# A SwiGLU down projection as seven block products in place of eight, and a zero fill on another queue

## The chip, the cores and the metric

One Trainium2 chip, one of its cores. The metric is the device time of the whole kernel in microseconds. A NeuronCore has five engines with a queue each: PE (TensorE, matmuls), DVE (VectorE), ACT (ScalarE), POOL (GpSimd) and SP (SyncE, which here only issues DMAs). ACT can issue DMAs too. PE writes into PSUM, which has eight banks of 128 x 512 floats; DVE and ACT take results out of it.

## The reference

Two transformer-like blocks follow each other on x, 1024 tokens by 1024 features, in float32. The first mixes by retention (8 heads) and a state space branch (S5), then by cross attention to 256 memory rows. The second mixes by four small mixers, one of them a gated delta rule, and ends in a SwiGLU layer and a norm. The change touches the last layer and, for its preparation, the retention:

```python
def swiglu(h, w_gate_up, w_down):
    gu = h @ w_gate_up
    gate, up = jnp.split(gu, 2, axis=-1)
    return (jax.nn.silu(gate) * up) @ w_down

x = x + swiglu(rmsnorm(x, norm2_w), w_gate_up, w_down)
return rmsnorm(x, final_norm_w)
```

The hidden width is 2816 = 22 x 128, so w_down has 2816 rows and 1024 columns.

## The kernel before, in words

**Products.** Every float32 operand of a large product is split into a high part (rounded to the matmul's format by ACT, L166, L181, L768) and a low part (the rest, by DVE, L167, L182, L769). `mm3` (L185) makes high x high, high x low and low x high, three matmuls (L187, L188, L189) of 128 x 128 weights by 512 columns, into one PSUM bank. Raw weights come through a ring of three buffers (`wraw`), the parts through rings of four (`whi`, `wlo`).

**Order.** Python generators are woven into each other and so give the order in which instructions are written down. From this, a scheduler with a model of the times makes a fixed order for each engine. An engine then takes its instructions in that order and waits at each for its semaphores; so do the DMA queues of SP and ACT.

**Retention** (L1097 and on). 32 steps m (four pairs of heads by eight chunks) interleave projections (`keys`, `values`), a transpose (`turn`), scores and outputs. At m = 0, 8, 16 and 24 `gates` (L1134) first makes two gate columns and loads the projection weights of the pair through `wraw`. The scan of the S5 branch (L1462 to L1464), a chain of small DVE instructions, runs beside it. At the start a zeroed tile is written to a DRAM buffer `t_d` by two DMAs of ACT's queue (L1112), each reading one tile of 129 columns 32 times. `t_d` is used far later, by the delta rule.

**Gate-up.** The product with w_gate_up is itself made of seven block products (`pair`, L802, with sums of weights from `prep`, L762, which is drawn one pair ahead; an even i is a gate, an odd i an up column pair). `finish` (L732) applies Silu to the gates (ACT), multiplies the up columns with them (POOL, L738) and stores the result, the hidden layer, to DRAM (`ff_d`, L740), 44 stores by SP.

**Down** (L842 to L878). The residual is loaded to `xk` (L843, eight DMAs of ACT's queue). The loop runs over f, two blocks of 128 rows of w_down at a time, 11 rounds. A round loads two blocks of the hidden layer (L849) and two of w_down (L177) by SP and splits them; then for each of 8 token tiles t and 2 halves c4 of the columns it makes 6 matmuls into a bank and adds the bank to `xk` (DVE, L864). In the last round each half is followed by a square with a row sum (ACT, L868) and the norm: POOL's power (L289), scaling by ACT (L876) and DVE (L877), and the output's DMA (L878).

Of the kernel before, what the change touches and what calls it, by code (L numbers as in the profile page):

```python
# [18 lines left out]
P = 128  # L19
# [103 lines left out]
class Kern:  # L123
# [482 lines left out]
    def stage2(self, x_d):  # L606
# [28 lines left out]
        ff_d = self.dram.tile([DFF, S], F32, name="ff_d")  # L635
# [96 lines left out]
        def finish(i, n, src):  # L732

            if i % 2 == 0:
                act.activation(src, src, AF.Silu)
                sg[n] = src
                return
            g.tensor_mul(src, src, sg[n])  # L738
            c, h = i // 2 * 2 + int(n[0]) - 1, int(n[1]) - 1
            nc.sync.dma_start(ff_d[c * P:(c + 1) * P, hs(h)], src)  # L740
# [7 lines left out]
        def add(i, n, other):  # L748

            def res(ps):  # L750
                tag, bufs = ("sg", 4) if i % 2 == 0 else ("nt" if i >= NEARLY else "sum", 2)
# [50 lines left out]
        def pair(i, w):  # L802
# [9 lines left out]
            yield from product(w["s2"], "t2", lambda ps: v.tensor_add(u2, ps, s1[i]))  # L812
            yield from product(w["s3"], "t3", lambda ps: v.tensor_add(u3, ps, u2))
# [17 lines left out]
        for i in range(NPAIR):  # L831
# [3 lines left out]
            self.drain(pair(i, w))  # L835
            w = w2


        NFT = 2
        fa = ArenaPool(self.slot(3, [P, 8192]), 2)  # L840
# [3 lines left out]
        for f0 in range(0, NF, NFT):  # L844
            fs = fa.tile([P, 2, NFT, S], F32R, tag="ff")
            ws = []
            for f in range(f0, f0 + NFT):
                r = self.wp.tile([P, S], F32, tag="wraw", name=self.nm("fraw"), bufs=3)
                nc.sync.dma_start(r, ff_d[f * P:(f + 1) * P])  # L849
                self.split(fs[:, 0, f - f0], fs[:, 1, f - f0], r)  # L850
                ws.append(self.weights([wd[f * P:(f + 1) * P]], 1))
            if f0 + NFT == NF:
                gb = self.wp.tile([P, NH, HT], F32, tag="wraw", name="gb", bufs=3)
                nc.scalar.dma_start(gb, I["final_norm_w_2"].rearrange("(o n c) -> o n c", o=1, n=NH).to_broadcast([P, NH, HT]))
            for t in range(KD):
                tok = slice(t * P, (t + 1) * P)
                if f0 + NFT == NF:
                    ms = self.wk.tile([P, 2], F32, tag="fms", name=self.nm("fms"))
                for c4 in range(2):
                    x = xk[:, t, c4]  # L860
                    ps = (self.pmm if c4 else pb).tile([P, HT], F32, tag="mm" if c4 else "b", name=self.nm("mm"))
# [1350 lines left out]
```

## Time and profile before

| what | us |
|---|---|
| median of 3 runs | 2501.27 (2499.54 to 2502.29) |
| the profiled execution, device time | 2498.12 |
| its span, first to last instruction | 2496.1 |
| PE busy in the span | 2418.4 (97%) |
| DVE, ACT, POOL busy | 1528.8, 827.3, 593.5 |
| mean granted TensorE clock | 0.989 of full speed |

All rows come from the profiled execution, whose times count from its first instruction. A row of the timeline gives start, duration, engine and line, what is written and read, and in brackets how long the engine stood idle before and what released it. "issue" as a releaser is time in which the engine waited for nothing that the profile shows. Tile names are those of the program; an arena has the name of its slot (s). A q behind an engine (SPq, ACTq) is its queue of DMA issues and semaphores.

### The profile page before, as it was taken

The numbers are of one execution on the slowest core, as the hardware profiler recorded it, in microseconds if no ns is written. First come the engines' busy times: TensorE is split into PE (matmuls) and PEld (weight loads), VectorE is DVE, ScalarE is ACT, GpSimd is POOL, SyncE is SP. The second block draws the span as 40 slices with busy tenths as digits, with TensorE's granted clock in tenths as the row PEclk, the third lists the DMA queues.
The fourth block names the chain that finished last, engine by engine and source line by source line (L and its number), as shares of the span: only waits on it lengthen the run. The fifth ranks groups of instructions, "written<-read, shape, count | busy, mean of one in ns | idle before, by whom it ended". The sixth has DMA issues, their size and how long they took to land.

```text
span 2496.1 us, 34790 instructions
## 1 busy us (share of the span) xinstructions
PE 2418.4 (97%) x13241; PEld 2026.5 (81%) x13241; DVE 1528.8 (61%) x2782; ACT 827.3 (33%) x1289; POOL 593.5 (24%) x538
## 2 busy tenths in 40 slices
PE   7998989999999999999999999999989999999998
PEld 7886779999977788888777788977868888888886
DVE  6456668934512775545785654367687666657777
ACT  6434311112112443444554322165443223221113
POOL 0006512322200441124635511043111111110002
PEclk9999999999999999999999999999999999999999
DMA  9745572112697444453346564236343222234332
GB/s 252 225 95 168 162 113 68 61 42 85 203 295 213 149 135 136 145 184 102 97 137 188 151 179 131 92 124 217 92 149 101 95 80 78 87 129 150 101 101 85
DMA packets 421382, 336.80 MB, mean 135 GB/s; under 512 B 46848, under 2 KB 364752, under 8 KB 420384
## 3 DMA queue, kind: packets, MB, share of 16 engines
q1 hardware_dynamic: 378960, 291.05, 38.5%
q10 hardware_dynamic: 42256, 43.52, 6.3%
q8 instruction: 105, 1.72, 0.3%
q14 instruction: 61, 0.50, 0.1%
HBM read 239.00 MB, written 95.52 MB: 134 GB/s over the span
## 4 chain that ended last, share of the span: by engine, by line
PE 80%; DVE 7%; DMA 4%; POOL 4%; issue 3%; ACT 2%; ACTq 1%; SPq 1%; POOLq 0%; DVEq 0%
PE mm L187 20%; PE mm L188 19%; PE mm L189 19%; PE qkv L187 3%; PE qkv L188 2%; PE qkv L189 2%; POOL m L1394 2%; PE yps L1085 1%; PE yps L1081 1%; DMA y<-y_d 1%; DVE wlo L182 1%; PE dz L2131 1%; DVE nt L308 1%; DVE s L310 1%; PE o L1200 1%
## 5 line engine op out<-in xcount | busy, mean ns | idle before, releaser
L187 PE MATMUL mm<-s,whi 128*128 128x512 f32 (+1 forms) x2112 | 833.9, 397 | 16.9 <-ACT sg L1137 6.3
L188 PE MATMUL mm<-s,whi 128*128 128x512 f32 (+1 forms) x2112 | 827.4, 392 | 2.2 <-DVE s L310 1.1
L189 PE MATMUL mm<-s,wlo 128*128 128x512 f32 (+1 forms) x2112 | 826.3, 392 | 2.2 <-DVE wlo L769 2.2
L187 PEld LDWEIGHTS mm<-s,whi 128*128 128x128 f32 x2112 | 400.8, 190 | 105.0 <-issue 6.9
L189 PEld LDWEIGHTS mm<-s,wlo 128*128 128x128 f32 x2112 | 401.4, 190 | 86.5 <-DVE wlo L769 3.5
L188 PEld LDWEIGHTS mm<-s,whi 128*128 128x128 f32 x2112 | 402.0, 190 | 82.4 <-issue 3.0
L182 DVE TENSOR_TENSOR wlo<-wraw,whi 128x1024 fp32r<-128x1024 f32 x204 | 280.4, 1376 | 184.1 <-ACT whi L181 179.5
L181 ACT ACTIVATE whi<-wraw 128x1024 fp32r<-128x1024 f32 x204 | 215.0, 1056 | 369.2 <-PE mm L188 197.7
L864 DVE TENSOR_TENSOR s<-mm,s 128x512 f32<-128x512 f32 x176 | 118.3, 688 | 66.9 <-PE mm L189 66.9
L738 POOL TENSOR_TENSOR c<-c,c 128x512 f32<-128x512 f32 x44 | 69.4, 1580 | 367.5 <-DVE c L753 213.8
L187 PE MATMUL mm<-whi,s 128*128 128x512 f32 (+1 forms) x416 | 155.3, 374 | 0.0
L188 PE MATMUL mm<-wlo,s 128*128 128x512 f32 (+1 forms) x416 | 155.2, 373 | 0.0
L189 PE MATMUL mm<-whi,s 128*128 128x512 f32 (+1 forms) x416 | 154.9, 373 | 0.0
L187 PE MATMUL qkv<-whi,s 128*128 128x256 f32 x512 | 152.2, 298 | 0.0
L188 PE MATMUL qkv<-wlo,s 128*128 128x256 f32 x512 | 147.5, 288 | 0.0
L189 PE MATMUL qkv<-whi,s 128*128 128x256 f32 x512 | 146.8, 287 | 0.0
L289 POOL TENSOR_TENSOR rs<-rv,mhalf 128x4 f32<-128x4 f32 (+3 forms) x47 | 49.2, 1047 | 228.8 <-DVE rv L287 212.5
L187 PEld LDWEIGHTS qkv<-whi,s 128*128 128x128 f32 x512 | 97.5, 190 | 4.7 <-issue 3.9
L768 ACT ACTIVATE whi<-wraw 128x1024 fp32r<-128x1024 f32 (+1 forms) x62 | 55.7, 907 | 135.5 <-PE mm L188 70.5
L188 PEld LDWEIGHTS qkv<-wlo,s 128*128 128x128 f32 x512 | 97.6, 191 | 0.9
L189 PEld LDWEIGHTS qkv<-whi,s 128*128 128x128 f32 x512 | 97.6, 191 | 0.3
L188 PEld LDWEIGHTS mm<-wlo,s 128*128 128x128 f32 x416 | 78.4, 188 | 13.8
(498 smaller groups left out, 3754.3 us busy)
## 6 DMA issues: line engine op xcount, KB each, us to landing
wraw<-in_w_in_dram SPq DMA_DIRECT2D x58, 512.0 KB
wraw<-in_w_out_dram SPq DMA_DIRECT2D x48, 512.0 KB
wraw<-in_w_gate_up_dram SPq DMA_DIRECT2D x48, 512.0 KB
ff_d<-c SPq DMA_DIRECT2D x44, 256.0 KB
fraw<-ff_d SPq DMA_DIRECT2D x22, 512.0 KB
wraw<-in_w_down_dram SPq DMA_DIRECT2D x22, 512.0 KB
s<-ret_d SPq DMA_DIRECT2D x16, 512.0 KB
s<-x_d SPq DMA_DIRECT2D x16, 512.0 KB
```

The costliest lines, as they stand in the source:

```text
L181: nc.scalar.activation(hi, raw, AF.Copy)
L182: nc.vector.tensor_sub(lo, raw, hi.bitcast(F32))
L187: mm(ps, ah, bh, start=start, stop=False)
L188: mm(ps, ah, bl, start=False, stop=False)
L189: mm(ps, al, bh, start=False, stop=stop)
L289: nc.gpsimd.tensor_tensor(r, v, self.mhalf[:, :1].to_broadcast([P, n]), op=ALU.pow)
L308: nc.vector.scalar_tensor_tensor(t[:, :n], src(k), g[:, k:k + 1], rb[:, :n], op0=ALU.mult, op1=ALU.mult)
L310: nc.vector.tensor_sub(lo[:, k, :n], t[:, :n], hi[:, k, :n].bitcast(F32))
L738: g.tensor_mul(src, src, sg[n])
L768: act.activation(d[0][:, s], src, AF.Copy)
L864: v.tensor_add(x, ps, x)
L1394: eng.tensor_tensor(out, a, b, op=ALU.mult)
```

## The change

Down is made of seven products of blocks instead of eight. w_down is cut by even and odd blocks of 128 rows and by halves of columns, the hidden layer by even and odd blocks and halves of tokens. Four sums of weights per pair of blocks (`down_sums`) are made by DVE during the retention, 11 steps, at the m listed in the diff, through the `wraw` ring, and stored to DRAM. Four sums of the hidden layer (t1 to t4) are made by DVE in the gate-up stage, after the third product of the pair that follows (`up_sums`), and stored by SP with three of the plain blocks, 77 stores in all. The new loop has the products outermost; each goes over 11 blocks in 6 steps (five of two blocks, one of one) and holds four PSUM banks, one per token tile of a half. Every step's operands are loaded from DRAM by SP and split (`down_loads`); two steps are kept ready, the first two before the last gate-up pair is over. `evac` adds each product to the outputs it belongs to. The norm's parts are made when a half is complete, for half of the tokens after the fifth product, for the others in the last, whose final two steps run tile by tile. The zero fill goes to SP, in eight DMAs at odd m from 5 on, from a tile of 1032 columns. The SBUF kept for descriptors of POOL's DMAs is set to 1024 bytes.

```diff
@@ -632,7 +632,8 @@
         self.wk = self.pool("wk2", 2)
         pt, pb = mx.pt, mx.pb
         xk_d = self.dram.tile([S, D], F32, name="xk_d")
-        ff_d = self.dram.tile([DFF, S], F32, name="ff_d")
+        ff_d = {n: self.dram.tile([DFF // 2 // P, P, HT], F32, name=f"ff_{n}")
+                for n in ("b11", "b21", "b22", "t1", "t2", "t3", "t4")}
         b_d = self.dram.tile([4, P, HT], F32, name="b_d")
         def turn_x(h):
@@ -736,8 +737,26 @@
                 sg[n] = src
                 return
             g.tensor_mul(src, src, sg[n])
-            c, h = i // 2 * 2 + int(n[0]) - 1, int(n[1]) - 1
-            nc.sync.dma_start(ff_d[c * P:(c + 1) * P, hs(h)], src)
+            up[i, n] = src
+            if n == "12":
+                pend.append(i)
+            else:
+                nc.sync.dma_start(ff_d["b" + n][i // 2], src)
+        up, pend = {}, []
+        def up_sums():
+            while pend:
+                i = pend.pop()
+                b11, b12, b21, b22 = (up.pop((i, n)) for n in ("11", "12", "21", "22"))
+                t2 = self.wk.tile([P, HT], F32, tag="ut2", name=self.nm("ut2"), bufs=1)
+                v.tensor_sub(b11, b12, b11)
+                v.tensor_sub(b12, b22, b12)
+                v.tensor_sub(t2, b22, b11)
+                v.tensor_sub(b21, b21, t2)
+                for n, t in (("t1", b11), ("t2", t2), ("t3", b12), ("t4", b21)):
+                    nc.sync.dma_start(ff_d[n][i // 2], t)
         def first(i, ps):
             tag = ("ssq0", "ssq1", "sq", "sq")[i % 4]
@@ -748,7 +767,7 @@
         def add(i, n, other):
             def res(ps):
-                tag, bufs = ("sg", 4) if i % 2 == 0 else ("nt" if i >= NEARLY else "sum", 2)
+                tag, bufs = ("sg", 4) if i % 2 == 0 else ("u" + n, 2 if n == "11" else 1)
                 c = self.wk.tile([P, HT], F32, tag=tag, name=self.nm("c"), bufs=bufs)
                 v.tensor_add(c, ps, other)
                 finish(i, n, c)
@@ -810,6 +829,7 @@
                 add(i, "22", u3)(ps)
                 v.tensor_add(u2, ps, u2)
             yield from product(w["s2"], "t2", lambda ps: v.tensor_add(u2, ps, s1[i]))
+            up_sums()
             yield from product(w["s3"], "t3", lambda ps: v.tensor_add(u3, ps, u2))
             yield from product(w["a22"], "t4", add(i, "21", u3))
             yield from product(w["s1"], "t1", fifth)
@@ -832,50 +852,115 @@
             if i + 1 < NPAIR:
                 w2 = prep(i + 1)
                 w2["rest"]()
-            self.drain(pair(i, w))
+            todo = pair(i, w)
+            if i + 1 == NPAIR:
+                self.drain(islice(todo, 4))
+                ld = self.down_loads(ff_d, wd)
+                ops = [next(ld) for _ in range(2)]
+            self.drain(todo)
             w = w2
-
-
-        NFT = 2
-        fa = ArenaPool(self.slot(3, [P, 8192]), 2)
+        up_sums()
+        self.down(ld, ops, xk_d, (self.pmm, "mm"), (pb, "b"), (pt, "tr"))
+    DOWN = (("a11", "b11"), ("a12", "b21"), ("s2", "t2"), ("s3", "t3"), ("a22", "t4"), ("s1", "t1"), ("s4", "b22"))
+    def down_loads(self, ff_d, wd):
+        nc = self.nc
+        ta = ArenaPool(self.slot(3, [P, 8192], F32))
+        wj = wd.rearrange("(j i p) (n c) -> i n p j c", i=2, p=P, n=2)
+        sw = self.sw_d.rearrange("i j p n c -> i n p j c")
+        at = {"a11": wj[0, 0], "a21": wj[0, 1], "a12": wj[1, 0], "a22": wj[1, 1],
+              "s2": sw[0, 0], "s3": sw[0, 1], "s4": sw[1, 0], "s1": sw[1, 1]}
+        for wn, xn in self.DOWN:
+            for j0 in range(0, 11, 2):
+                n = min(2, 11 - j0)
+                r = ta.tile([P, 2, HT], tag="traw", name=self.nm("traw"), bufs=2)[:, :n]
+                nc.sync.dma_start(r, ff_d[xn][j0:j0 + n].rearrange("j p c -> p j c"))
+                t = ta.tile([P, 2, 2, HT], F32R, tag="ts", name=self.nm("ts"), bufs=3)
+                raw = self.wp.tile([P, 2, HT], F32, tag="wraw", name=self.nm("wraw"), bufs=3)[:, :n]
+                nc.sync.dma_start(raw, at[wn][:, j0:j0 + n])
+                hi, lo = (self.wp.tile([P, 2, HT], F32R, tag=q, name=self.nm(q), bufs=4)[:, :n] for q in ("whi", "wlo"))
+                self.split(t[:, 0, :n], t[:, 1, :n], r)
+                self.split(hi, lo, raw)
+                yield t[:, 0], t[:, 1], hi, lo, n
+    def down(self, ld, ops, xk_d, *banks):
+        nc, v, act, g = self.nc, self.nc.vector, self.nc.scalar, self.nc.gpsimd
         xk = self.slot(2, [P, KD, NH, HT], F32)
         for t in range(KD):
             nc.scalar.dma_start(xk[:, t], xk_d[t * P:(t + 1) * P].rearrange("p (n c) -> p n c", n=NH))
-        for f0 in range(0, NF, NFT):
...
+        ac = Arena(self.slot(1, [P, 8192], F32))
+        gb, s1, u3 = ac.take((NH, HT)), ac.take((4, HT)), ac.take((4, HT))
+        nc.scalar.dma_start(gb, self.ins["final_norm_w_2"].rearrange("(o n c) -> o n c", o=1, n=NH).to_broadcast([P, NH, HT]))
+        ms = {}
+        def done(t, c):
+            x = xk[:, t, c]
+            last = t in ms
+            if not last:
+                ms[t] = ac.take((2,))
+            jk = self.wk.tile([P, HT], F32, tag="sg", name=self.nm("jk"), bufs=4)
+            act.activation(jk, x, AF.Square, accum_out=ms[t][:, c:c + 1])
+            if not last:
+                g.tensor_tensor(x, x, gb[:, c], op=ALU.mult)
+                return
+            m = self.wk.tile([P, 1], F32, tag="fm", name=self.nm("fm"))
+            v.tensor_add(m, ms[t][:, 0:1], ms[t][:, 1:2])
+            r = self.rstd_from(m, 1, 1.0 / D, "lrs")
+            act.activation(xk[:, t, 1 - c], xk[:, t, 1 - c], AF.Copy, scale=r)
+            v.scalar_tensor_tensor(x, x, r, gb[:, c], op0=ALU.mult, op1=ALU.mult)
+            nc.sync.dma_start(self.out[0, t * P:(t + 1) * P].rearrange("p (n c) -> p n c", n=NH), xk[:, t])
+        def add(t, c, other, last=True):
+            v.tensor_add(xk[:, t, c], other, xk[:, t, c])
+            if last:
+                done(t, c)
+        def evac(p, t, ps):
+            if p == 0:
+                act.activation(s1[:, t], ps, AF.Copy)
+                add(t, 0, s1[:, t], False)
+            elif p == 1:
+                add(t, 0, ps)
+            elif p == 2:
+                v.tensor_add(s1[:, t], ps, s1[:, t])
+            elif p == 3:
+                v.tensor_add(u3[:, t], ps, s1[:, t])
+                add(t, 1, u3[:, t], False)
+                add(t + 4, 1, u3[:, t], False)
+            elif p == 4:
+                add(t, 1, ps)
+            elif p == 5:
+                add(t + 4, 1, ps)
+                v.tensor_add(s1[:, t], ps, s1[:, t])
+                add(t + 4, 0, s1[:, t], False)
+            else:
+                add(t + 4, 0, ps)
+        NSTEP = 6
+        for p in range(len(self.DOWN)):
+            bank = [banks[0], banks[1], banks[2], banks[p % 2]]
+            ps = [b.tile([P, HT], F32, tag=tag, name=self.nm("mm")) for b, tag in bank]
+            def mms(t, i, op):
+                th, tl, wh, wl, n = op
                 tok = slice(t * P, (t + 1) * P)
...
+                for k in range(n):
+                    self.mm3(ps[t], th[:, k, tok], tl[:, k, tok], wh[:, k], wl[:, k], i == 0 and k == 0, i == NSTEP - 1 and k == n - 1)
+            final = p + 1 == len(self.DOWN)
+            for i in range(NSTEP - 2 * final):
+                op = ops.pop(0)
+                for t in range(4):
+                    mms(t, i, op)
+                ops += [o for o in [next(ld, None)] if o]
+            for t in range(4):
+                if final:
+                    for i, op in enumerate(ops):
+                        mms(t, NSTEP - 2 + i, op)
+                evac(p, t, ps[t])
 @@ -1106,11 +1191,15 @@
         self.load_consts(r1, "causalT", "inv")
         self.t_d = self.dram.tile([2, 8, 4, P + 1, P], F32, name="t_d")
-        zero = r1.tile([P, P + 1], F32, name="zero")
+        zero = r1.tile([P, 8 * (P + 1)], F32, name="zero")
         g.memset(zero, 0.0)
-        for i in range(2):
-            nc.scalar.dma_start(self.t_d[i].rearrange("n h s c -> (n h s c)").rearrange("(p a b) -> p a b", p=P, b=P + 1),
-                                zero.unsqueeze(1).to_broadcast([P, 32, P + 1]))
+        def zeros():
+            for i in range(2):
+                for n in range(0, 8, 2):
+                    nc.sync.dma_start(self.t_d[i, n:n + 2].rearrange("n h s c -> (n h s c)").rearrange("(p b) -> p b", p=P), zero)
+                    yield
+        zeros = zeros()
         cosb = r1.tile([P, 8, 32], F32, name="cosb")
         sinb = r1.tile([P, 8, 2, 32], F32, name="sinb")
         with ExitStack() as c:
@@ -1242,6 +1331,7 @@
                 for i, t in enumerate((hi, lo)):
                     nc.sync.dma_start(ret_d[i, ch * P:(ch + 1) * P, h * HT:(h + 1) * HT], t.bitcast(F32))
+        sums = self.down_sums()
         M = 32
         for m in range(M + 1):
             if m < M:
@@ -1258,8 +1348,30 @@
                 turn(m)
             if m and m % 4 == 0:
                 finish(m // 4 - 1)
+            if m % 2 and 5 <= m:
+                next(zeros, None)
+            if m in (10, 11, 12, 13, 14, 18, 19, 20, 21, 22, 26):
+                next(sums)
             if m == 29:
                 reload()
+    def down_sums(self):
+        nc, v = self.nc, self.nc.vector
+        wd = self.ins["w_down_2"][0]
+        self.sw_d = self.dram.tile([2, 11, P, NH, HT], F32, name="sw_d")
+        for j in range(11):
+            e, o = (self.wp.tile([P, NH, HT], F32, tag="wraw", name=self.nm("wdr"), bufs=3) for _ in range(2))
+            for i, t in enumerate((e, o)):
+                f = 2 * j + i
+                nc.sync.dma_start(t.rearrange("p n c -> p (n c)"), wd[f * P:(f + 1) * P])
+            v.tensor_add(o[:, 1], e[:, 1], o[:, 1])
+            v.tensor_sub(e[:, 1], e[:, 0], e[:, 1])
+            v.tensor_sub(e[:, 0], o[:, 1], e[:, 0])
+            v.tensor_sub(o[:, 0], o[:, 0], e[:, 0])
+            for i, t in enumerate((e, o)):
+                nc.sync.dma_start(self.sw_d[i, j], t)
+            yield
 
     def cmul(self, eng, o, a, b, t, conj_sign=1):
@@ -2196,7 +2308,7 @@
     import concourse.bacc as bacc
     from concourse.bass_utils import run_bass_kernel_spmd
-    nc = bacc.Bacc("TRN2", target_bir_lowering=False, num_devices=1)
+    nc = bacc.Bacc("TRN2", target_bir_lowering=False, num_devices=1, dynamic_dma_scratch_size=1024)
     consts, cols = shape_constants()
     arrays, aps = {}, {}
     for name in _INS + ["consts"]:
```

## Rows read from the trace of the kernel before

**Rows 1.** the page's first part: busy us (share of the span) and instructions
```profile
PE 2418.4 (97%) x13241; PEld 2026.5 (81%) x13241; DVE 1528.8 (61%) x2782; ACT 827.3 (33%) x1289; POOL 593.5 (24%) x538
```

**Rows 2.** groups by line, 2220 to 2500 us: busy us, mean ns | idle before, releaser
```profile
L188 PE MATMUL mm<-wlo,s 128*128 128x512 f32 x352 | 137.1, 389 | 0.0
L864 DVE TENSOR_TENSOR s<-mm,s 128x512 f32<-128x512 f32 x176 | 118.3, 688 | 66.9 <-PE mm L189 66.9
L167 DVE TENSOR_TENSOR s<-fraw,s 128x1024 fp32r<-128x1024 f32 x22 | 26.8, 1216 | 2.9 <-ACT s L166 2.9
```

**Rows 3.** timeline of PE, first and last matmul of the down stage: start us, us, ...
```profile
2245.39 0.39 PE L187 MATMUL mm<-whi,s 128*128 128x512 f32 x1
...
2484.53 0.39 PE L189 MATMUL mm<-whi,s 128*128 128x512 f32 x1
```

**Rows 4.** timeline of ACT, 295 to 370 us (ACTq: its DMA queue)
```profile
309.94 14.70 ACTq L1112 DMA_DIRECT2D t_d<-zero  x2
324.69 1.06 ACT L181 ACTIVATE whi<-wraw 128x1024 fp32r<-128x1024 f32 x1 [16.80 <-issue]
339.27 1.57 ACT L1137 ACTIVATE sg<-mm 128x512 f32<-128x512 f32 x3 [6.98 <-issue]
```

**Rows 5.** DMA in all, 661 to 680 us: loads of x_d and w_out
```profile
DMA packets 5937, 5.58 MB, mean 294 GB/s; under 512 B 160, under 2 KB 4239, under 8 KB 5936
```

**Rows 6.** timeline: two loads of 512 KB and the ACT instruction that each released
```profile
2235.29 0.32 SPq L849 DMA_DIRECT2D fraw<-ff_d  x1
2246.01 1.06 ACT L166 ACTIVATE s<-fraw 128x1024 fp32r<-128x1024 f32 x1 [11.23 <-DMA fraw<-ff_d]
...
2443.29 0.33 SPq L177 DMA_DIRECT2D wraw<-in_w_down_dram  x1
2447.09 1.06 ACT L181 ACTIVATE whi<-wraw 128x1024 fp32r<-128x1024 f32 x1 [3.60 <-DMA wraw<-in_w_down_dram]
```

**Rows 7.** timeline of all engines at the end, 2484 to 2497 us
```profile
2489.60 0.61 ACT L868 ACTIVATE jk<-s 128x512 f32<-128x512 f32 x1
2491.69 0.75 DVE L877 SCALAR_TENSOR_TENSOR s<-s,rs,gb 128x512 f32<-128x512 f32 x1 [0.72 <-POOL rs L289]
```

**Rows 8.** stretches: us, PE, PEld, DVE, ACT, POOL busy (x), PEclk, DMA share, GB/s
```profile
1945.00:2050.00 105.00, 105.00 (x464) 86.99 (x464) 68.12 (x89) 32.45 (x47) 14.24 (x10) 1.00 0.26 81
```

**Rows 9.** groups by line and shape, DVE, 1830 to 2224 us
```profile
L769 DVE TENSOR_TENSOR wlo<-a,whi 128x512 fp32r<-128x512 f32 x22 | 23.8, 1081 | 0.1
L769 DVE TENSOR_TENSOR wlo<-wraw,whi 128x512 fp32r<-128x512 f32 x22 | 15.0, 682 | 0.0
```

**Rows 10.** waits, 1830 to 2224 us: in total us, times, longest
```profile
DVE a L783 <- DMA wraw<-in_w_gate_up_dram: 35.5, 19, 2.9
```

**Rows 11.** timeline of PE, 316 to 348 us, around the two gaps
```profile
323.14 0.39 PE L189 MATMUL mm<-s,wlo 128*128 128x512 f32 x1
326.29 0.76 PE L187 MATMUL mm<-s,whi 128*128 128x512 f32 x1 [2.76 <-ACT g L479]
333.25 0.39 PE L189 MATMUL mm<-s,wlo 128*128 128x512 f32 x1
339.92 0.79 PE L187 MATMUL mm<-s,whi 128*128 128x512 f32 x1 [6.28 <-ACT sg L1137]
```

**Rows 12.** stretches, as Rows 8, of the retention's start
```profile
340.00:345.00 5.00, 5.00 (x15) 3.98 (x16) 4.26 (x18) 0.84 (x2) 0.00 (x0) 0.66 1.16 186
```

**Rows 13.** DMA queue of ACT, 332 to 339.3 us: packets, MB, share of 16 engines
```profile
q10 hardware_dynamic: 1069, 0.55, 69.1%
```

**Rows 14.** timeline of all engines, 446 to 457 us, one step of the retention
```profile
449.77 0.28 DVE L1182 TENSOR_TENSOR qk<-tr,consts 128x128 f32<-128x128 f32 x1
450.84 0.60 PE L1189 MATMUL sc<-qk 128*128 128x256 f32 x2
```

**Rows 15.** timeline of ACT, 400 to 530 us, one step m apart
```profile
452.24 0.38 ACT L1170 ACTIVATE vs<-qkv 128x256 f32<-128x256 f32 x1 [5.48 <-PE qkv L189]
460.07 0.38 ACT L1170 ACTIVATE vs<-qkv 128x256 f32<-128x256 f32 x1 [7.45 <-PE qkv L189]
```

More of the change, by code (lines that the diff above doesn't have):

```diff
@@ L843, in stage2 @@
             nc.scalar.dma_start(xk[:, t], xk_d[t * P:(t + 1) * P].rearrange("p (n c) -> p n c", n=NH))
-        for f0 in range(0, NF, NFT):
[L845 to L855, printed above, removed]
-                tok = slice(t * P, (t + 1) * P)
[L857 to L861, printed above, removed]
-                    for f, (wh, wl) in enumerate(ws):
-                        self.mm3(ps, fs[:, 0, f, tok], fs[:, 1, f, tok], wh[:, 0, hs(c4)], wl[:, 0, hs(c4)], f == 0, f == NFT - 1)
-                    v.tensor_add(x, ps, x)
-                    if f0 + NFT < NF:
-                        continue
-                    jk = self.wk.tile([P, HT], F32, tag="sg", name=self.nm("jk"), bufs=4)
-                    act.activation(jk, x, AF.Square, accum_out=ms[:, c4:c4 + 1])
-                    if c4 == 0:
-                        g.tensor_tensor(x, x, gb[:, c4], op=ALU.mult)
-                if f0 + NFT < NF:
-                    continue
-                m = self.wk.tile([P, 1], F32, tag="fm", name=self.nm("fm"))
-                v.tensor_add(m, ms[:, 0:1], ms[:, 1:2])
-                r = self.rstd_from(m, 1, 1.0 / D, "lrs")
-                act.activation(xk[:, t, 0], xk[:, t, 0], AF.Copy, scale=r)
-                v.scalar_tensor_tensor(xk[:, t, 1], xk[:, t, 1], r, gb[:, 1], op0=ALU.mult, op1=ALU.mult)
-                nc.sync.dma_start(self.out[0, tok].rearrange("p (n c) -> p n c", n=NH), xk[:, t])
```

## The prediction

> **What bounds the kernel now.** I read the page first: PE is busy 97% of the span [rows 1], so the question in each stage is which PE time goes and whether anything else becomes late. The groups of the last stage, the down projection, come next [rows 2]: three matmul lines of 352 each, 1056 in all, with no idle time in front of them, while DVE waits 66.9 us for PE in its sum out of PSUM (L864). PE sets the pace there. The timeline gives the pace: from 2245.39, the first start, to 2484.53, the last, are 1055 steps [rows 3], so (2484.53 - 2245.39) / 1055 = 0.2267 us per matmul (a row's 0.39 us overlaps the next one's). The stage ends with a stretch that has no matmul: the last one is over at 2484.53 + 0.39 = 2484.92, the span at 2496.1, so 11.2 us follow, in which DVE, ACT and POOL catch up on norms that came faster than they could be served, and the last output lands.
>
> **The products.** Before, 22 blocks of f, 8 token tiles, 2 halves and 3 matmuls make 1056. After, 7 products, 11 blocks, 4 token tiles and 3 make 924, of the same shape (128x128 by 512). 132 fewer at 0.2267 us: **-29.9 us**, the whole stage 209.5 us instead of 239.4, if PE stays the bound.
>
> Can the operands come in time? A step (two blocks, 24 matmuls) takes 5.44 us, and with the short sixth step the 42 steps take 209.5 / 42 = 4.99 us on average. For it ACT makes two high parts of 1.06 us [rows 4], DVE two low parts of 1.22 us [rows 2]. Per product DVE has 11 x 1.22 = 13.4 us of these and at most 12 sums of 0.69 us (8.3 us), 21.7 of 29.9 us. Bytes: 7 x 11 x 512 KB = 40.4 MB in 209.5 us, 193 GB/s. The loads of x_d and w_out, most of them in packets under 2 KB, ran at 294 GB/s [rows 5]. The tight place is the ring of two raw buffers: a buffer turns round in issue 0.33 + landing L + ACT 1.06 + DVE 1.22, so the ring gives a step every (2.6 + L) / 2 us and holds PE up where L is over 7.4 us. A 512 KB load landed in 3.8 us (2443.29 to 2447.09) beside one other load, and in 10.7 us (2235.29 to 2246.01) beside the 4 MB of the residual xk [rows 6]. I take 3.8 us for the stage, 3.2 us per step, so hidden. The residual and the broadcast of the norm's weights are still loaded at the start, just when steps 2 and 3 are fetched; two steps are prefetched, which is 10.9 us of cover against 10.7 us of landing and some 4 us of splitting. Floor 0, ceiling 8 us; I take **+3 us**.
>
> PSUM: four banks per product, and eight exist for two products, so the next product starts while the last is emptied: nothing.
>
> **The tail.** The last product finishes one token tile after another, 9 matmuls or 2.04 us apart, and only four tiles are left to norm. Per tile DVE needs the sum 0.69, two of a single column and the scaling 0.75 [rows 2, 7], under 2.04 us; so nothing piles up. After the last matmul: sum 0.69, then square to the end of the scaling as in the last tile of before, 2489.60 to 2492.44 = 2.84 us [rows 7], then the output's landing, 2496.1 - 2492.44 = 3.7 us: 7.2 us for 11.2. **-4.0 us**.
>
> **Sums beside the gate-up products.** 44 subtractions go to DVE, 33 stores more to SP. DVE is busy 68.12 of 105 us there [rows 8]. A subtraction without company takes 0.68 us, the same shape beside POOL 1.08 us [rows 9]: 30 to 48 us over 22 pairs of 84 matmuls (19.0 us each, 419 us), 7 to 11% more. The cover is the pair of lead that the weights have (19 us) and six PSUM banks for products of 2.72 us. On SP the four new stores wait for DVE, and the next pair's weight load stands behind them; these loads already keep DVE waiting 1.9 us each (35.5 / 19) [rows 10], with no wait on PE. Were that cover gone, each odd pair would pay some 4 us, 44 us in all; I take **+1 us** (0 to 5).
>
> **The zero fill.** Before, ACT's queue issues two zero DMAs in 516-byte pieces, 8192 of them, and is held 14.70 us, from 309.94 to 324.64; its next work starts at 324.69 [rows 4]. PE needs ACT to empty PSUM and stands from 323.53 to 326.29, then again from 333.64 to 339.92 [rows 11]: 2.76 and 6.28 us. After such a gap PE runs at the granted clock 0.66 of the mean, its 1.2 GHz level for part of the stretch: 15 matmuls in 5 us where 22 fit [rows 12], 7 x 0.2267 = 1.6 us, twice. In all 9.04 + 3.2 = 12.2 us. The first gap surely goes. In the second, ACT waited 6.98 us for nothing the profile names [rows 4], while its queue's zero pieces still filled 69.1% of the engines' time [rows 13]; I read it as something ACT itself fetched that stood behind them, and let it go too: **-12.2 us** (floor of the gain 4.4, the first gap alone). The Trainium skill (DMA: Bandwidth & Descriptors, Queues, rings and completion order) says that each DMA engine takes the queues in turn, a packet at a time. By that rule any other fetch is slowed as long as the fill runs, and the sum is this one; without it, it is 7.8 us less.
>
> On SP the fill is 8 issues of 128 pieces of 4128 bytes. At the rate of before, 14.70 / 8192 per piece, that is 1.8 us of SP in all; behind them stand only stores of finished heads and, later, weights. The larger memset (eight times 129 columns) is on POOL, off the path. The smaller descriptor memory concerns DMAs issued by POOL, and the program has none. Both: nothing.
>
> **Sums of w_down in the retention.** New on the path: 11 steps, each with two loads and two stores of 512 KB and four DVE sums. They draw on two things. (a) DVE. It is nearly full around 450 us, PE just fed: the rotated keys are ready at 449.77 + 0.28 = 450.05, the matmul that reads them starts at 450.84 [rows 14], 0.8 us of slack. Four sums are 2.7 us, beside POOL 4.3 us [rows 9], and DVE stands in front of a late load 1.9 us more [rows 10]. At best each falls into gaps (0), at worst a step costs PE 4.3 + 1.9 - 0.8 = 5.4 us, 59 us in all. The scan's small instructions already fill the same gaps without a wait on PE, so I stay near the floor: 0.3 us a step, 3 us. The Trainium skill (SBUF - State Buffer, Who interferes with whom) says that a DVE instruction with two SBUF inputs and a GpSimd one that reads SBUF shut each other out. The two rows of one shape, 1081 and 682 ns, bear this out; by it a step is 4.3 us of DVE, by the rows alone 2.7 to 4.3 us. (b) The ring of three raw buffers, shared with the weights. A step turns round in load 0.33 + 3.8, sums 2.8, store 0.33 + 3.8 = 11.0 us, but the steps are one per m, 460.07 - 452.24 = 7.8 us apart [rows 15]. Five steps need 55 us and have six m's, 47 us; the gate weights that follow at m = 16 and 24, fetched long ahead before, come up to 8 us late each. Prefetching into the free buffer takes most of it: 2.5 us each (0 to 8), 5 us. Together **+8 us**.
>
> **Sum.** -29.9 + 3 - 4.0 + 1 - 12.2 + 8 = -34.1 us. The profiled execution took 2498.1 us (span 2496.1), the median of three runs is 2501.3; I count from the median, 3.2 us above the profiled one: **2467 us**. This measurement tells differences over 0.2%, 5 us.
>
> **Rivals.**
> *A, the supply loop (slower than before).* In the down stage loads land as slowly as beside xk, 10.7 us, because two queued loads per step, a serial raw ring and the split follow each other. Then a step takes (2.6 + 10.7) / 2 = 6.65 us, 1.66 more than PE needs, 42 times: +70 us, 2537 us. It decides from L = 7.4 us; at 9.0 us the gain is gone. For it: one landing of 10.7 us. Against: 3.8 us without the big transfer, 294 GB/s where 193 are needed. Chance 0.07.
> *B, the retention pays.* DVE delays cost 2 us a step (22) and both gates wait 6 us (12): 34 instead of 8, 2493 us. For it: 0.8 us of slack, 11.0 against 7.8 us. Against: PE waits for nobody there now, and loads may be issued early. Chance 0.16.
> *C, the move does not do what it is said to do.* Only the first gap closes; ACT's silent 6.98 us has another cause. 7.8 us less gain: 2475 us. Chance 0.13.
> The forecast has 0.62; 0.02 is left for what I do not see.
>
> **Numbers.** The fast end is the sum without the four costs, 46.1 us below: 2455. The slow end takes in C and nearly B: 2490. A and half of B stay outside, under 2 in 10. Faster by over 0.2%: forecast, C and most of B, 0.88; within: 0.03 (the heavy end of B); slower: A, the worst of (a) and the rest, 0.09.
>
> **What would show it.** Right: 924 matmuls 0.2267 us apart with no wait at L of the new loads; some 7 us from the last matmul to the end; no gap at 323 and 334 us; PE unbroken at m = 16 and 24. Wrong: PE waiting on the low parts (ts, wlo) in the down stage (A); PE waiting on DVE or on whi around 450 to 600 us, DVE waiting on the wdr loads (B); ACT silent after the sine (C).

## The result, and the profile after

The changed kernel takes **2464.08 us** (median of 4 runs, 2461.16 to 2465.93) against 2501.78 us for the kernel before, timed beside it (4 runs): a ratio of **0.9845, interval 0.9831 to 0.9859**. In a second set of runs it was 2461.92 us and 0.9846 (0.9823 to 0.9869). The forecast was 2467 us in a range of 2455 to 2490. The profiled execution took 2462.94 us, its span is 2461.1 us, 35.0 us less than before; the steps below are counted in spans.

The first part of the page, which answers to [rows 1]; columns as there:

```profile
PE 2388.0 (97%) x13109; PEld 1998.9 (81%) x13109; DVE 1527.8 (62%) x2778; ACT 863.5 (35%) x1333; POOL 598.5 (24%) x538
```

PE has 132 instructions less, as it should. Where the time went shows when the same points are laid beside each other in both timelines (us; a minus is a gain):

| stretch | before | after | difference |
|---|---|---|---|
| start to first projection matmul of the retention | 347.14 | 336.48 | -10.7 |
| from there to the wait on `sig`, at 829.80 and 824.93 | 482.66 | 488.45 | +5.8 |
| from there to the first matmul of down | 1415.59 | 1418.83 | +3.2 |
| first to last matmul of down | 239.14 | 209.22 | -29.9 |
| last matmul to the end of the span | 11.6 | 8.1 | -3.5 |

(The last row counts from the start of that matmul.) The sum is -35.1 us, the span's -35.0.

**Down.** The groups by line of the changed kernel, 2180 to 2465 us; they answer to [rows 2]:

```profile
L187 PE MATMUL mm<-whi,s 128*128 128x512 f32 x308 | 119.8, 389 | 0.0
L188 PE MATMUL mm<-wlo,s 128*128 128x512 f32 x308 | 119.8, 389 | 0.0
L189 PE MATMUL mm<-whi,s 128*128 128x512 f32 x308 | 119.6, 389 | 0.0
L166 ACT ACTIVATE s<-s 128x1024 fp32r<-128x1024 f32 (+1 forms) x42 | 41.6, 990 | 108.7 <-PE mm L188 87.6 <-issue 8.7 <-DMA s<-ff_b 6.2
```

Three times 308 matmuls are 924, with no idle time in front of any. ACT, which makes the high parts of the hidden layer, waits for PE to release a buffer (87.6 us) and only 6.2 us for loads: supply leads, PE sets the pace. The first and last of them on PE's timeline, as in [rows 3]:

```profile
2243.76 0.39 PE L187 MATMUL mm<-whi,s 128*128 128x512 f32 x1
...
2452.98 0.39 PE L189 MATMUL mm<-whi,s 128*128 128x512 f32 x1
```

923 steps in 209.22 us are 0.2267 us each, the pace of before. The last matmul is over at 2453.37, 7.7 us before the span ends. In between stands one tile's sum, square and norm (timeline of all engines; answers to [rows 7]):

```profile
2453.58 0.68 DVE L918 TENSOR_TENSOR s<-mm,s 128x512 f32<-128x512 f32 x1
2454.35 0.63 ACT L906 ACTIVATE jk<-s 128x512 f32<-128x512 f32 x1 [0.80 <-DVE rv L287]
2456.77 0.75 DVE L914 SCALAR_TENSOR_TENSOR s<-s,rs,s 128x512 f32<-128x512 f32 x1 [0.72 <-POOL rs L289]
```

**The zero fill.** The timelines of SP and of ACT, 310 to 345 us (the idle time and its end in brackets; compare [rows 4]):

```profile
312.56 6.75 SPq L1200 DMA_DIRECT2D t_d<-zero  x8
319.41 0.99 SPq L480 DMA_DIRECT2D sg_d<-g  x1
```

```profile
314.69 1.06 ACT L181 ACTIVATE whi<-wraw 128x1024 fp32r<-128x1024 f32 x1 [4.57 <-PE mm L188]
329.28 1.09 ACT L1226 ACTIVATE sg<-mm 128x512 f32<-128x512 f32 x2 [2.65 <-DMA sg_d<-g]
```

The scheduler put all eight DMAs at the start, not at the odd m where they are written. PE has no gap here: 37.0 of 37 us busy from 310 to 347, where the kernel before has the two gaps of [rows 11]. And the first Silu of the gates, silent for 6.98 us in [rows 4], now has a named releaser, the landing of SP's store of `g`.

**The retention.** The waits of DVE for the sums of w_down (instructions that use the tile `wdr`; us, times), and PE's first new gap:

```profile
  DMA wdr<-in_w_down_dram: 19.9, 9
```

```profile
437.21 0.30 PE L1266 MATMUL tr<-consts,ra 128*128 128x128 f32 x1 [0.46 <-DVE gt L1327]
```

Three such gaps, 0.46, 0.97 and 0.55 us, each ended by DVE, are new; PE is not held up at m = 16 and 24.

### The profile page after: what moved, and what is told of

Its sections match the earlier page's. It is cut to its first block, busy times and chain, and to the rows that moved or that the text cites. A ratio compares the mean times of both kernels' runs of the same rounds, so it can differ in the third digit from the quotient of the medians.

```text
span 2461.1 us, 34716 instructions
## 1 busy us (share of the span) xinstructions
PE 2388.0 (97%) x13109; PEld 1998.9 (81%) x13109; DVE 1527.8 (62%) x2778; ACT 863.5 (35%) x1333; POOL 598.5 (24%) x538
## 4 chain that ended last, share of the span: by engine, by line
PE 73%; DVE 9%; DMA 8%; POOL 4%; issue 3%; ACT 2%; SPq 1%; ACTq 0%; POOLq 0%; DVEq 0%
PE mm L187 19%; PE mm L188 19%; PE mm L189 19%; POOL m L1506 2%; PE qkv L187 2%; DMA wdr<-in_w_down_dram 2%; PE qkv L188 1%; PE qkv L189 1%; DVE wlo L182 1%; PE yps L1170 1%; DMA sw_d<-wdr 1%; PE dz L2243 1%; DMA wraw<-in_w_gate_up_dram 1%; PE gob L1821 1%; DVE s L310 1%
## 5 line engine op out<-in xcount | busy, mean ns | idle before, releaser
L182 DVE TENSOR_TENSOR wlo<-wraw,whi 128x1024 fp32r<-128x1024 f32 x182 | 252.1, 1386 | 157.1 <-ACT whi L181 153.0
L181 ACT ACTIVATE whi<-wraw 128x1024 fp32r<-128x1024 f32 x182 | 191.8, 1056 | 313.5 <-PE mm L188 186.9
L187 PE MATMUL mm<-whi,s 128*128 128x512 f32 (+1 forms) x372 | 138.2, 371 | 0.0
L188 PE MATMUL mm<-wlo,s 128*128 128x512 f32 (+1 forms) x372 | 137.9, 371 | 0.0
L189 PE MATMUL mm<-whi,s 128*128 128x512 f32 (+1 forms) x372 | 137.8, 371 | 0.0
L166 ACT ACTIVATE s<-s 128x1024 fp32r<-128x1024 f32 (+1 forms) x62 | 54.2, 874 | 136.6 <-PE mm L188 87.6
L167 DVE TENSOR_TENSOR s<-s 128x1024 fp32r<-128x1024 f32 (+1 forms) x50 | 54.6, 1092 | 63.5 <-ACT s L166 57.6
```

The costliest lines, as they stand in the source:

```text
L166: self.nc.scalar.activation(hi, src, AF.Copy)
L167: (lo_engine or self.nc.vector).tensor_sub(lo, src, hi.bitcast(F32))
L181: nc.scalar.activation(hi, raw, AF.Copy)
L182: nc.vector.tensor_sub(lo, raw, hi.bitcast(F32))
L187: mm(ps, ah, bh, start=start, stop=False)
L188: mm(ps, ah, bl, start=False, stop=False)
```

## The experiments

Ratios are to the kernel before, timed on the same chip in the same set; the changed kernel's own is 0.9845 and 0.9846. The scheduler writes a new order for every edit, so an edit also shifts gaps of 1 to 4 us in stages that it does not touch. For terms of a few us I therefore read the trace at the nearest point behind the edit, and the total beside it.

### The zero fill: back, alone, in larger pieces, in small pieces on SP

Put back into the changed kernel:

```diff
-        zero = r1.tile([P, 8 * (P + 1)], F32, name="zero")
+        zero = r1.tile([P, P + 1], F32, name="zero")
...
-                    nc.sync.dma_start(self.t_d[i, n:n + 2].rearrange("n h s c -> (n h s c)").rearrange("(p b) -> p b", p=P), zero)
...
+            nc.scalar.dma_start(self.t_d[i].rearrange("n h s c -> (n h s c)").rearrange("(p a b) -> p a b", p=P, b=P + 1),
+                                zero.unsqueeze(1).to_broadcast([P, 32, P + 1]))
```

> The changed kernel with the zero fill alone put back: two DMAs of ACT's queue in 516-byte pieces from a tile of 129 columns. Theory (ACT is held by the issue and its next fetch stands behind the pieces; both gaps of PE and the slow clock after each are the fill's): PE stands again some 2.8 and 6.3 us near 323 and 334 us, and the kernel is 10 to 12 us slower than the changed one, about 2475 us. Rival C (the second gap has another cause): 3 to 5 us slower, about 2468 us.

2481.32 us, ratio 0.9915 (0.9899 to 0.9930). PE's two gaps are back, 2.44 and 8.79 us, and the first projection matmul is at 349.54, **13.1 us** later than in the changed kernel (336.48). The total is some 17 us later, more than the 10 to 12 expected; beyond the 13.1, gaps of 3.13 us at 714 and 2.46 us at 1873 stand where the changed kernel has 0.92 and 1.11 us, by my reading a matter of the new order.

Alone in the kernel before, the same lines the other way round (the tile, `zeros` and its call in the loop over m are those of the change):

```diff
-        zero = r1.tile([P, P + 1], F32, name="zero")
+        zero = r1.tile([P, 8 * (P + 1)], F32, name="zero")
...
+            if m % 2 and 5 <= m:
+                next(zeros, None)
```

> The kernel before with the zero fill alone as in the changed kernel (eight DMAs of SP in 4128-byte pieces, tile of 1032 columns). Theory: 10 to 12 us faster than before, about 2490 us, no gap of PE near 323 and 334 us. Rival C: 3 to 5 us faster, about 2497 us, with PE still waiting some 6 us for ACT near 334 us.

2492.71 us, ratio 0.9958 (0.9943 to 0.9973): 10.3 us. The first projection matmul is at 334.38 for 347.14, **12.8 us** earlier. Rival C is out from both sides.

Then the queue is kept and only the pieces are made larger:

```diff
-        zero = r1.tile([P, P + 1], F32, name="zero")
+        zero = r1.tile([P, 8 * (P + 1)], F32, name="zero")
...
-                                zero.unsqueeze(1).to_broadcast([P, 32, P + 1]))
+                                zero.unsqueeze(1).to_broadcast([P, 4, 8 * (P + 1)]))
```

> The kernel before with the zero fill still in two DMAs of ACT's queue, but read from a tile of 1032 columns, so that the pieces are 4128 bytes (1024 in all, not 8192). Theory (the hold goes by the number of pieces, 14.7 us / 8192 each): ACT's queue is held about 1.8 us, both gaps of PE close nearly, and 9 to 12 us are gained without a change of queue. Rival (what counts is that ACT's queue issues it at all, or the bytes): the issue stays near 14 us or ACT still stands still after it, and the gain is under 4 us.

2491.65 us, ratio 0.9948 (0.9929 to 0.9967), the same as with the move. ACT's queue on the timeline of ACT, against 14.70 us in [rows 4]:

```profile
310.87 1.91 ACTq L1112 DMA_DIRECT2D t_d<-zero  x2
```

These are 0.65 us for the first DMA and 1.23 us for the second. In the kernel before the first took 0.64 us too, with its 4096 pieces, and the second 14.03 us. So the hold is not a price per piece, by which I had worked out 1.8 us for SP. The packets tell what ends it: when the second issue was over, 5223 of the 8192 small pieces had still to start (5365 and 5492 in the two other kernels that have them), while of the 1024 large ones here none had started. The queue takes some 5200 to 5500 pieces ahead in these runs and then waits until earlier ones have moved. PE has no gap from 300 to 420 us, and the first projection matmul is at 334.36. **So the move of the queue, by which the change is described, is not what pays: the larger pieces are.** The last run turns this round, with the small pieces on the other queue:

```diff
-            nc.scalar.dma_start(self.t_d[i].rearrange("n h s c -> (n h s c)").rearrange("(p a b) -> p a b", p=P, b=P + 1),
+            nc.sync.dma_start(self.t_d[i].rearrange("n h s c -> (n h s c)").rearrange("(p a b) -> p a b", p=P, b=P + 1),
```

> The kernel before with its two zero DMAs in 516-byte pieces moved to SP's queue as they are. Theory (two costs: the issue holds the queue that does it for 14 us, and the pieces fill the DMA engines so that SP's store of the gate g lands late and ACT's next Silu, which takes over g's memory, waits for it): ACT is free, so the first gap of 2.76 us goes, but SP is held in its place, and its store and the next weights stand behind the fill: PE still waits 5 us or more for them, and the kernel is between 3 us faster and 10 us slower than before. Rival (ACT's hold is the whole cost): both gaps close and 10 to 12 us are gained, as with the large pieces.

2516.40 us, ratio 1.0050 (1.0031 to 1.0070): 12.6 us slower than before, worse than I gave it. The mechanism of the theory holds, its size was too small: I had not reckoned with how long the store behind the fill would take to issue. SP's timeline, 300 to 400 us:

```profile
309.60 14.04 SPq L1112 DMA_DIRECT2D t_d<-zero  x2
323.69 15.00 SPq L480 DMA_DIRECT2D sg_d<-g  x1
338.74 24.18 SPq L177 DMA_DIRECT2D wraw<-in_w_in_dram  x4
```

and ACT's and PE's in the same stretch:

```profile
351.74 1.58 ACT L1137 ACTIVATE sg<-mm 128x512 f32<-128x512 f32 x3 [27.58 <-DMA sg_d<-g]
```

```profile
352.39 0.80 PE L187 MATMUL mm<-s,whi 128*128 128x512 f32 x1 [23.67 <-ACT sg L1137]
```

The chain is plain here: pieces, the issue of the store of `g` (15.00 us), its landing, the Silu, PE. One gap of 23.67 us stands where the kernel before has 9.04 us in two.

This also explains the silent 6.98 us of [rows 4]. In the kernel before SP issued that store here:

```profile
326.26 0.32 SPq L480 DMA_DIRECT2D sg_d<-g  x1
```

The semaphore that tells of its landing is complete at 339.20, and the Silu that waits for it starts at 339.27. The DMA queues from 314 to 332 us in the kernel before (packets, MB, time as a share of 16 engines; ACT's queue is q10, SP's q1):

```profile
q10 hardware_dynamic: 4886, 2.81, 122.3%
```

It is the only queue in the answer: SP's moved nothing until 333. In the changed kernel, in the same stretch, the fill is among SP's own packets:

```profile
DMA packets 3503, 6.36 MB, mean 353 GB/s; under 512 B 196, under 2 KB 2233, under 8 KB 3502
...
q1 hardware_dynamic: 3369, 5.54, 83.8%
```

353 GB/s against 156 GB/s in the kernel before.

### The sums of w_down in the retention

Without them (the down stage reads plain blocks, `wj`, in place of `sw`):

```diff
-            if m in (10, 11, 12, 13, 14, 18, 19, 20, 21, 22, 26):
-                next(sums)
```

> The changed kernel without the sums of w_down in the retention: none is loaded, made or stored, and the down stage reads plain blocks of w_down in their place (this leaves out the weight sums). It prices the term that the prediction put at 8 us. The theory from the two traces (three new PE gaps of 2.0 us, a few slower stretches): 4 to 6 us faster than the changed kernel, about 2459 us. Rival (the delay is absorbed behind the retention, where PE waits for something else anyway): under 2 us. Rival B's size (34 us) would need 2430 us.

2459.60 us, ratio 0.9834 (0.9813 to 0.9854). Loads and stores kept, only DVE's work left out:

```diff
-            v.tensor_add(o[:, 1], e[:, 1], o[:, 1])
-            v.tensor_sub(e[:, 1], e[:, 0], e[:, 1])
-            v.tensor_sub(e[:, 0], o[:, 1], e[:, 0])
-            v.tensor_sub(o[:, 0], o[:, 0], e[:, 0])
```

> The changed kernel with the loads and stores of the sums of w_down kept and the four DVE operations of each step left out (plain blocks are stored in place of the sums). It divides the 4.5 us that all of it cost: if DVE is the cost, as much is gained as without the whole step, 4 to 5 us; if the ring and the transfers are, 0 to 1 us. The prediction had 3 us for DVE and 5 us for the ring.

2460.83 us, ratio 0.9833 (0.9813 to 0.9852). The totals lie inside each other's intervals and those of the changed kernel. Two stretches from the first projection matmul tell more, one to the last scores matmul (`sc`), where the retention ends, and one to the wait on `sig`:

| kernel | sums | to the last `sc`, us | to `sig`, us |
|---|---|---|---|
| before; with the new fill; large pieces on ACT; small pieces on SP | none | 324.44 in each | 482.7; 484.4; 487.8; 484.2 |
| changed, no sums | none | 324.44 | 484.3 |
| changed, transfers without DVE's work | transfers only | 324.44 | 483.4 |
| changed, two profiles; one raw buffer (below) | all | 328.45, 327.92; 328.51 | 488.5, 487.4; 487.8 |
| fill put back; no sums beside gate-up | all | 329.03; 328.06 | 491.3; 491.5 |
| sums later (below) | all | 328.64 | 491.5 |

The last `sc` on PE's timeline, with the transfers alone (first projection matmul at 336.83),

```profile
661.27 0.59 PE L1278 MATMUL sc<-qk 128*128 128x256 f32 x2
```

and in the changed kernel (336.48):

```profile
664.93 0.59 PE L1278 MATMUL sc<-qk 128*128 128x256 f32 x2
```

In all rows but the last the same 2382 matmuls lie in the first stretch. It takes 324.44 us in six kernels, with the transfers alone too, and 327.92 to 329.03 us with DVE's work: **DVE is the whole cost there, 3.5 to 4.6 us, and the ring costs nothing**. The new gaps are 2.0 of the 4.0 us in the changed kernel; where the other half goes is open. What the second stretch adds is less even, and it does not go by the sums: the kernel with large pieces on ACT's queue has none and a gap of 4.08 us at 695 that waits for `ret_d`, and the three kernels with 491 us have gaps of 1.3 to 3.1 us between 698 and 760, for loads or, once, for ACT. Such gaps are as large as the term.

Later, where DVE has room:

```diff
-            if m in (10, 11, 12, 13, 14, 18, 19, 20, 21, 22, 26):
+            if m in (17, 18, 19, 20, 21, 22, 23, 25, 26, 27, 28):
```

> The changed kernel with the eleven steps of sums of w_down at m = 17 to 23 and 25 to 28 in place of 10 to 14, 18 to 22 and 26. After 500 us DVE is busy 17 to 23 of 50 us, before it 43 to 47. Theory (the sums cost PE time because DVE is full while the scan runs): the three new gaps of PE go, 2 to 4 us faster than the changed kernel, about 2461 us. Rival (the ring of raw buffers costs it, or the order of the work changes anyway): no gain, or up to 5 us slower, with PE waiting for the weights of m = 24.

2463.49 us, ratio 0.9837 (0.9816 to 0.9859): no gain beside 2461.92 us of the changed kernel in the same set. From 400 to 500 us PE is now busy without a break (stretches; columns as [rows 8]),

```profile
400.00:450.00 50.00, 50.00 (x341) 45.55 (x340) 44.12 (x159) 6.83 (x12) 10.86 (x18) 1.00 0.21 66
600.00:650.00 50.00, 49.36 (x396) 46.42 (x395) 30.22 (x88) 4.95 (x11) 18.39 (x28) 1.00 0.75 253
```

but from 600 to 650 the DMA engines are now busy 0.75 of the time (0.34 in the changed kernel), and what follows waits for loads (timeline of PE):

```profile
698.50 0.68 PE L1166 MATMUL yps<-oU,TZ 128*128 128x128 f32 x4 [1.35 <-DMA s<-ret_d]
...
760.48 0.68 PE L1166 MATMUL yps<-oU,TZ 128*128 128x128 f32 x4 [2.24 <-DMA TZ<-k_d]
```

Neither wait is that long in the changed kernel. To the last `sc` this kernel takes 4.2 us more than one without sums; 8 matmuls more lie before it in this order, 1.8 us at 0.2267 us each. So by this estimate the later sums still cost some 2.4 us there, and what that saves is lost behind it. The rival's "the order of the work changes anyway" is nearer, though PE waits for these loads and not for the weights of m = 24.

### The supply of the down stage

```diff
-                r = ta.tile([P, 2, HT], tag="traw", name=self.nm("traw"), bufs=2)[:, :n]
+                r = ta.tile([P, 2, HT], tag="traw", name=self.nm("traw"), bufs=1)[:, :n]
```

> The changed kernel with one raw buffer for the hidden layer in the down stage in place of two. It tests the supply loop by which rival A was worked out. If a buffer turns round in issue 0.33 + landing 3.8 + ACT 1.06 + DVE 1.22 = 6.4 us and PE needs a step every 4.99 us, the stage is 42 x 1.4 = 59 us longer, about 2523 us, with PE waiting on the hidden layer's parts. Rival (landing is much under 3.8 us once the ring is not kept waiting by a full queue, or the three slots of split parts give enough lead): under 10 us, about 2464 to 2474 us.

2519.26 us, ratio 1.0057 (1.0034 to 1.0079): 55 us slower than the changed kernel and slower than before. Down lasts from 2243.63 to 2503.20, 259.6 us against 209.6, so 50 us more; the tail is 3.4 us longer. A turn of the one buffer, on the timelines of SP, ACT and DVE:

```profile
2382.03 0.36 SPq L879 DMA_DIRECT2D s<-ff_t  x1
...
2386.32 1.06 ACT L166 ACTIVATE s<-s 128x1024 fp32r<-128x1024 f32 x1 [2.77 <-DMA s<-ff_t]
...
2387.41 1.22 DVE L167 TENSOR_TENSOR s<-s 128x1024 fp32r<-128x1024 f32 x1 [1.40 <-ACT s L166]
...
2388.66 0.36 SPq L879 DMA_DIRECT2D s<-ff_t  x1
```

6.63 us from issue to issue, for 6.4 in the model; the short sixth steps are quicker, so the stage has 259.6 / 42 = 6.18 us a step. The group of the first of three matmul lines, 2225 to 2514 us, says who was waited for, and that this time it is the bound:

```profile
L187 PE MATMUL mm<-whi,s 128*128 128x512 f32 x308 | 125.4, 407 | 31.5 <-ACT s L166 31.4
...
L189 PE MATMUL mm<-whi,s 128*128 128x512 f32 x308 | 102.2, 395 | 4.3 <-DVE s L167 4.3
```

31.5 + 4.3 = 35.8 us of the 50 are idle time in front of matmuls; the rest lies in the matmuls, of which the first after a gap takes 0.50 us and more for 0.39, and which run at a lower granted clock in places (0.89 of the mean from 2480 to 2490 us, behind a stretch of 10 us in which PE was busy 6.82). The loop of rival A is thus real, and two buffers keep it out of the way: 6.63 / 2 = 3.3 us a step, where PE needs 4.99.

### The sums beside gate-up

```diff
-                v.tensor_sub(b11, b12, b11)
-                v.tensor_sub(b12, b22, b12)
-                v.tensor_sub(t2, b22, b11)
-                v.tensor_sub(b21, b21, t2)
-                for n, t in (("t1", b11), ("t2", t2), ("t3", b12), ("t4", b21)):
+                for n, t in (("t1", b11), ("t2", b22), ("t3", b12), ("t4", b21)):
```

> The changed kernel with the four subtractions of the hidden layer per pair left out (plain blocks are stored in place of t1 to t4, and the third takes no tile of its own); all stores stay. It prices the DVE part of the term that the prediction put at 1 us (0 to 5). Theory: DVE has room there, 0 to 2 us faster than the changed kernel. Rival (the sums delay the weights' low parts at the odd pairs): 4 us at a pair, up to 44 us faster.

2463.95 us, ratio 0.9838 (0.9816 to 0.9861): nothing. From the gap that opens the stage to the first matmul of down it takes 2246.11 - 1843.24 = 402.9 us, the changed kernel 2243.76 - 1841.55 = 402.2.

The changed kernel, once more beside the last runs:

> The changed kernel as it is, as the measure for the two runs above on the same chip: 2464 us, a ratio to before of 0.985.

2461.92 us, as expected. No variant beats it by more than the intervals.

## Why the prediction was right, step by step

- **Products, -29.9 us: -29.9 us measured.** 132 matmuls at the pace of before, no gap in the stage.
- **Operands at the start of down, +3 us (0 to 8): 0.** ACT stood 7.64 us before it split the third step's load of the hidden layer at 2245.04, and nothing is named for that wait: its own queue was issuing the loads of `xk`, the last until 2244.99. But the first step's matmuls, from 2243.76, were then just beginning, and PE had no gap. Two prefetched steps were cover enough.
- **A misread row behind this term and rival A.** The 10.7 us of [rows 6] are no landing. The load issued at 2235.29 had landed at 2239.03 by its semaphore, 3.7 us later. ACT split it only at 2246.01 because its queue, which takes issues and work in one order, stood at the loads of `xk`:

```profile
2245.64 0.33 ACTq L843 DMA_DIRECT2D s<-xk_d  x1
```

  This issue waited for the semaphore of the *next* load of the hidden layer, issued at 2238.15 and landed at 2245.61, and it is this load that the row names as releaser, under the same tile name. Beside `xk` a load thus took 7.5 us in the kernel before; in the changed kernel it was 7.2 us (2236.47 to 2243.68). That is close to the 7.4 us from which A decides, but it holds only while `xk` is loaded.
- **Tail, -4.0 us: -3.5 us** (7.7 us left, for 7.2 worked out).
- **Sums beside gate-up, +1 us: 0** by the run without them. Gate-up opens with gaps of 2.51, 1.84 and 1.11 us, 5.5 us in all, where the kernel before has six of 0.61 to 1.07 us, 4.7 in all; they are there without the sums too (2.35, 1.84, 1.73 us), so they come from something else in the change, by my reading the new order of the work, which was not tried. The price of a sum beside POOL was misread: 1.08 us in [rows 9] is the mean of 14 instructions of 0.68 to 0.69 us and 8 of 1.77 to 1.78 us; the 8 are those that a product of POOL (L738) overlapped, for 1.23 us.
- **Zero fill, -12.2 us: -12.8 us alone, -13.1 us in the changed kernel.** The size is right, including the slow stretch after each gap. Two reasons behind it were not. I wrote that the second gap was "something ACT itself fetched that stood behind them"; it was SP's store of `g`, whose memory the next Silu takes over: that Silu's releaser is the store in the changed kernel and, at 27.58 us, with the small pieces on SP, and in the kernel before it starts 0.07 us after the store has landed. And I let the queue be the cause, as the change does; the run with larger pieces on ACT's own queue gained the same. The issue costs on SP were too low as well: eight issues held SP 6.75 us, not 1.8, without harm.
- The Trainium skill (DMA: Bandwidth & Descriptors, Queues, rings and completion order), which I had called in for this, says that a DMA engine takes the queues in turn. The trace does not show this for the first 6.7 us: issued at 326.26, SP's store moved no packet until 333, with ACT's queue alone filling the engines at 122.3%; only from 334 did both move. What held the store back in between no run isolates.
- **Retention, +8 us: some 4 us.** The term was oversized, and wrongly divided: of "(a) DVE 3, (b) ring 5" the first measured 3.5 to 4.6 and the second 0. POOL hardly slowed the sums of w_down: each of the four took 0.68 to 0.69 us in the median. In (b) I had written that "Prefetching into the free buffer takes most of it" and still charged 2.5 us to each gate; the loads of m = 16 and 24 never held PE up.
- **Sum.** -34.1 us forecast, -35.0 us in the spans and -37.7 us in the medians. It is closer than its terms: as the runs price them they give -29.9 + 0 - 3.5 + 0 - 12.8 + 4 = -42.2 us, 7.2 us more than the span shows. The first table has them: 2.1 us up to the first projection matmul (-10.7 for -12.8), 1.8 us on the way from there to `sig` (5.8 for 4), 3.2 us from `sig` to down. The first is there before the fill begins (ACT makes a `g` at 309.53 that it made at 307.29 before) and the second lies behind the last `sc`. By my reading they are gaps that the new order of the work shifts, as in the experiments; no run isolates them. My costs that were too high, 3 + 1 + 4 us, stood in for them by chance.
- **The rivals.** A's loop is real, but its 10.7 us were no landing, and it needs one buffer less to come true: then the kernel takes 2519 us. B's 34 us are out, the whole of the sums is worth 4; the signs that I gave for B came all the same (PE waiting on DVE, DVE waiting 19.9 us for `wdr`), so they tell that the mechanism is there and not its size. C is refuted twice.

## What to carry to other kernels

When a DMA holds its queue and everything beside it, count its pieces before moving it: here eight times larger pieces on the same queue gave all of the gain, and the small pieces on another queue made it worse than before. A stage that PE bounds with no gap can be priced by its matmuls to a tenth of a us, provided the turn of its smallest buffer ring stays under the time of a step; work out that turn and test it by taking one buffer away. Terms of 1 to 5 us in a kernel whose order a scheduler writes are read at the next common point of the timelines, not from totals: the sums of w_down stood out at the end of their own stage and were blurred 150 us later. Before a wait in front of an instruction is taken for a landing, look at what the same engine was issuing.

## What the runs showed of the hardware

- Two DMAs of 4096 pieces of 516 bytes held the queue that issued them 14.0 to 14.7 us, on ACT and on SP alike, nearly all of it the second; of 512 pieces of 4128 bytes, 1.9 us. When the hold ended, 5223 to 5492 of the 8192 small pieces had still to start, in three kernels.
- While the small pieces ran the DMA engines were full at some 130 GB/s (0.94 MB from 324.7 to 332 us); the stretch with the larger ones moved 353 GB/s.
- Behind such a fill on the same queue the issue of a 256 KB store took 15.00 us; in the kernel before it took 0.32 us (at 326.26), and the store then landed only at 339.20.
- ACT takes its DMA issues and its work in one order: an issue at 2245.64 that waited for a load's landing kept it from an operand that had landed at 2239.03.
- A DVE instruction of 0.68 us (L769, `wlo` from `a`) took 1.77 to 1.78 us the 8 times of 22 that a product of POOL overlapped it, for 1.23 us; 8 of the same shape (`wlo` from `wraw`) that one overlapped for 0.46 to 0.52 us kept 0.68 us.
